# Products of constants in three idle places of TensorE, and the sample scores of the decay attention bound behind the fourth pair's first work

## The chip, the cores and the metric

The program runs on one core of one Trainium2 chip. Its engines work side by side, each through a queue of its own in program order: TensorE (PE; its weight loads are listed as PEld), VectorE (DVE), ScalarE (ACT), GpSimd (POOL), and SyncE (SP), which here only issues DMA transfers. The metric is the device time of one execution in microseconds (us), the median over runs. The profile also gives TensorE's granted clock, as a share of full speed: it is seen at two levels, 1.0 (2.4 GHz) and 0.5 (1.2 GHz).

## The reference

One encoder layer in fp32 for two requests that share weights: a prompt of 1024 tokens, and a sample of 64 tokens that comes with caches (256 past tokens of attention, 256 memory tokens, recurrent states). Model width is 1024. Cut to its frame:

```python
x = layer_norm(x)
proj = x @ w_in                                   # three mixers read the same projection
mixed = concat(gla(...), s5(...), fox(...)) @ w_mix_out
x = layer_norm(alpha * x + mixed)
x = layer_norm(alpha * x + mem_attend(x, mem_k, mem_v, w_q, w_o))
x = layer_norm(alpha * x + conv_ffn(x, w_up, conv_w, conv_b, w_down))
```

and the mixer that matters here, the decay attention (8 heads of 64):

```python
s = einsum('bqhd,bkhd->bhqk', q, k) * 64 ** -0.5
s = s + F[q] - F[k]                               # F: cumulative log-forget values
s = where(k_pos <= q_pos, s, -inf)
out = einsum('bhqk,bkhd->bqhd', softmax(s), v)
```

The sample's 64 queries attend to 256 cached keys and their own 64. All the prompt's and sample's outputs, new keys, values and states are returned.

## The kernel before

**Precision and stages.** fp32 products are made from rounded parts: `mm3` (L198) issues three products hi x hi, hi x lo, lo x hi. A weight tile is loaded raw by SP (L117), rounded by ACT (L118, `_hi`), and the remainder is taken by DVE or POOL (L119, `_lo`). In order of time the stages are: input and memory projections, GLA and S5 (to about 415 us), decay attention (415 to 570), mixing projection with its norm (560 to 680), memory attention (690 to 912), its output projection, the up-projection (to about 1440), and the down-projection.

**Decay attention.** The prompt's eight heads go as four pairs, p = 0 to 3 (z is the head in the pair), each in eight query tiles i of 128. A tile has scores `fx_s` (L983, L984, with the diagonal mask added as a product of `maskb` by `identb`, a bf16 identity, L986), a DVE reduction that adds the decay and finds the extreme value (L989), ACT's exponential (L991), transposes `fx_t` (L998), their copies `fx_pt` (L1000, L1002), products with V `fx_po` (L1007), and an ACT copy to `mixT` (L1009). V of a pair is loaded by L965. After a pair's tiles, `fx_rl` (L1015) spreads the reciprocal row sums and L1017 multiplies `mixT` by them.

**Sample scores.** `fox_sample` is a generator: the code calls it once at p = 2 for its loads (`FsD` and `qk` through SP, L912 and L915) and for the addition of a mask to the decay values (L917, DVE), and then at p = 3, tiles 0, 2, 4 and 6, once for each pair of sample heads: `fs_s` (12 products on L925 to L927), reduction L929, exponential L931, scaling L932 and L933, transposes `fs_t` (L936), `fs_o` (L942), copy to `mixT` (L944).

**Mixing projection.** `residual` adds `mixT` times `w_mix_out` to x, in two stages of 512 inputs. A stage has four weight tiles, u = 0 to 3; a token tile takes 24 products `ps_o`, six for each u. Its input x is loaded into `Xa` and `Xb` (L1078) over the storage that the decay attention used. `bo` holds the rounded parts of `mixT` (L1041, L1042); after stage 0 DVE adds the sums to x (L1057), after stage 1 a norm follows, which squares on ACT (L139) over the tile of sums, and transposes x into features (`ps_tr`, L189).

**Memory attention.** `mem_sample(h)` runs one head of the sample: `ms_s` (L1139), softmax (L1098 to L1102), transposes `ms_t` (L1144), `ms_o` (L1150).

**Order and banks.** The instructions' order on every engine is made by a scheduler that simulates the program; `tc.issue_after` binds an instruction behind another without a wait. TensorE's sums live in eight banks: tag D (two buffers of two banks: `fx_s`, `ps_o`), tag T (two of one: `fx_t`, `m_s`), and tags E and F, one bank each, given in turn by

```python
def pse(name="pse", tag=None):
    turn[0] ^= 1
    return psum.tile([128, 512], F32, tag=tag or "EF"[turn[0]], name=name)
```

unless the caller names one (`fs_*` always E; `fx_po` and `fx_rl` always F).

## Time and profile before

| what | value |
|---|---|
| median of 3 runs | 1747.13 us (1738.27 to 1749.47) |
| the profiled execution | 1746.15 us, span 1744.4 us |
| mean granted TensorE clock | 0.979 |
| busy share of the span | PE 95%, DVE 61%, ACT 40%, POOL 40% |
| PE, products | 10856 |
| chain of waits that ended last | PE 44%, DVE 8%, issue 4%, POOL, ACT and DMA 2% each |

The busy share is an average over stages. A row of a timeline gives the start, the duration, the engine, the line and operation, and in brackets how long the engine had been idle before it and what ended that. "x4" groups four instructions in a row; products of one group overlap, so the spacing from start to start is what one costs. The chain of waits follows the end of the program backwards and gives each step's engine.

### The profile page before, as it was taken

The page shows a single profiled execution, that of the slowest core. Times are in us where ns is not written, and L with a number is a line of the kernel's source. Part 1 is how long each engine was busy: PE and PEld are TensorE (multiplying, and loading weights), DVE is VectorE, ACT ScalarE, POOL GpSimd, SP SyncE. Part 2 cuts the span into 40 slices and gives each one's busy share as a digit, 9 for nine tenths or more (in the row PEclk, how much of TensorE's full clock was granted, in tenths as well). Part 3 has the DMA queues.
Part 4 walks back from the last instruction along what each step waited for, and adds up shares of the span by engine and source line. Part 5 has one row for each costly group of instructions (what it writes and reads, how often), then busy time and mean ns, then how long its engine had stood idle before and what let it go on. Part 6 is the DMA issues. An engine that isn't in the chain of part 4 may idle for free.

```text
span 1744.4 us, 27851 instructions
## 1 busy us (share of the span) xinstructions
PE 1651.9 (95%) x10856; PEld 1451.6 (83%) x10856; DVE 1057.6 (61%) x1806; ACT 695.3 (40%) x1280; POOL 698.9 (40%) x748
## 2 busy tenths in 40 slices
PE   7799998998999999999989899999999998999997
PEld 5699986777777878998778799999999997767775
DVE  8754522674556236124445999778888876775547
ACT  6412224423555135225336654444444446121111
POOL 4454833020010267113223375545455547653323
PEclk9799999999999999999999899999999999999999
DMA  9640233438941311122112122222222226531112
GB/s 329 253 77 27 78 104 110 160 96 225 262 118 47 131 48 37 39 63 69 37 49 78 71 64 90 80 81 80 75 75 81 75 94 256 188 106 37 48 53 99
DMA packets 95753, 178.29 MB, mean 102 GB/s; under 512 B 26206, under 2 KB 48574, under 8 KB 95494
## 3 DMA queue, kind: packets, MB, share of 16 engines
q1 hardware_dynamic: 67910, 142.82, 26.9%
q10 hardware_dynamic: 27712, 33.70, 5.4%
q8 instruction: 85, 1.39, 0.3%
q14 instruction: 46, 0.38, 0.1%
HBM read 129.56 MB, written 46.34 MB: 101 GB/s over the span
## 4 chain that ended last, share of the span: by engine, by line
PE 44%; DVE 8%; issue 4%; POOL 2%; ACT 2%; DMA 2%; POOLq 0%; SPq 0%; DVEq 0%; ACTq 0%
PE u_a L1414 7%; PE ps_d L198 7%; PE u_d L1414 6%; PE u_c L1414 6%; PE ps_a L216 6%; PE ps_o L198 5%; PE u_b L1414 3%; PE m_o L198 1%; POOL wd_lo L119 1%; PE m_s L198 1%; DVE Yb L1580 1%; DVE y L1487 1%; DVE Ya L1580 1%; DMA hraw<-hD 1%; DMA kv_p<-out_mem_v_p 1%
## 5 line engine op out<-in xcount | busy, mean ns | idle before, releaser
L198 PE MATMUL ps_d<-wd_hi,hb 128*128 128x512 f32 x704 | 225.1, 396 | 11.3 <-DVE Ya L1580 3.5
L198 PEld LDWEIGHTS ps_d<-wd_hi,hb 128*128 128x128 f32 x704 | 132.1, 188 | 47.9 <-DVE Yb L1580 3.9
L1414 PE MATMUL u_a<-x2A,wu_wlo 128*128 128x288 f32 (+1 forms) x1032 | 138.6, 290 | 2.7 <-DVE x2A L1225 2.0
L198 PE MATMUL ps_d<-wd_lo,hb 128*128 128x512 f32 x352 | 139.0, 395 | 1.3 <-POOL wd_lo L119 1.3
L1414 PEld LDWEIGHTS u_a<-x2A,wu_wlo 128*128 128x128 f32 x1032 | 133.4, 192 | 3.3 <-DVE x2A L1225 2.4
L198 PE MATMUL ps_o<-wo_hi,bo 128*128 128x512 f32 x384 | 126.5, 403 | 3.0 <-ACT ps_o L139 2.7
L1360 POOL TENSOR_TENSOR wu_wlo<-wu_raw,wu_wlo 128x512 fp32r<-128x512 f32 x63 | 97.2, 1546 | 79.9 <-ACT wu_wlo L1359 79.9
L1487 DVE SCALAR_TENSOR_TENSOR y<-x2B,ffp,y 128x1024 f32<-128x1024 f32 x88 | 125.9, 1431 | 1.1 <-ACT y L1485 1.1
L1517 POOL TENSOR_TENSOR hb<-hraw,hb 128x1024 fp32r<-128x1024 f32 (+1 forms) x40 | 64.9, 1640 | 84.6 <-ACT hb L1516 84.6
L1360 POOL TENSOR_TENSOR wu_whi<-wu_whi 128x512 fp32r<-128x512 f32 x44 | 70.5, 1602 | 60.8 <-ACT wu_whi L1359 60.1
L198 PE MATMUL ps_b<-wb_hi,x0h 128*128 128x512 f32 (+2 forms) x256 | 89.5, 350 | 1.0 <-ACT fv_st L264 1.0
L1359 ACT ACTIVATE wu_wlo<-wu_raw 128x512 fp32r<-128x512 f32 x86 | 54.1, 631 | 90.7 <-DVE wu_raw L1356 39.3
L198 PEld LDWEIGHTS ps_o<-wo_hi,bo 128*128 128x128 f32 x384 | 72.7, 191 | 20.0 <-ACT ps_o L139 3.1
L198 PE MATMUL ps_b<-wb_lo,x0h 128*128 128x512 f32 (+2 forms) x256 | 88.4, 346 | 0.4 <-POOL wb_lo L119 0.4
L198 PE MATMUL ps_b<-wb_hi,x0l 128*128 128x512 f32 (+2 forms) x256 | 88.6, 346 | 0.0
L1580 DVE TENSOR_TENSOR Ya<-Ya,ps_d 128x1024 f32<-128x1024 f32 (+1 forms) x50 | 60.9, 1218 | 44.6 <-PE ps_d L198 39.1
L1042 POOL TENSOR_TENSOR bo<-mixT,bo 128x512 fp32r<-128x512 f32 (+1 forms) x18 | 22.7, 1273 | 151.6 <-ACT bo L1041 151.6
L119 POOL TENSOR_TENSOR wo_lo<-wo_raw,wo_hi 128x1024 fp32r<-128x1024 f32 x14 | 33.2, 2383 | 118.5 <-ACT fx_pt L1000 45.6
L198 PEld LDWEIGHTS ps_d<-wd_lo,hb 128*128 128x128 f32 x352 | 66.1, 188 | 16.9 <-POOL wd_lo L119 2.2
L119 POOL TENSOR_TENSOR wa_lo<-wa_raw,wa_hi 128x1024 fp32r<-128x1024 f32 x16 | 39.2, 2454 | 101.0 <-ACT wa_hi L118 67.8
L198 PE MATMUL ps_o<-wo_lo,bo 128*128 128x512 f32 x192 | 77.1, 402 | 1.1 <-POOL wo_lo L119 1.1
L1516 ACT ACTIVATE hb<-hraw 128x1024 fp32r<-128x1024 f32 (+1 forms) x40 | 25.3, 653 | 128.5 <-PE ps_d L198 116.2
(560 smaller groups left out, 4473.6 us busy)
## 6 DMA issues: line engine op xcount, KB each, us to landing
wu_raw<-in_w_up SPq DMA_DIRECT2D x88, 256.0 KB, 2.8
hD<-y ACTq DMA_DIRECT2D x22, 512.0 KB, 2.6
wd_raw<-in_w_dn SPq DMA_DIRECT2D x22, 512.0 KB, 3.5
hraw<-hD SPq DMA_DIRECT2D x20, 544.0 KB, 4.7
fx<-qk SPq DMA_DIRECT2D x28, 256.0 KB, 8.8
fxk<-qk SPq DMA_DIRECT2D x20, 256.0 KB, 4.8
wa_raw<-in_w_a SPq DMA_DIRECT2D x8, 512.0 KB, 3.7
stage<-in_w_mv SPq DMA_DIRECT2D x8, 512.0 KB, 8.4
```

The costliest lines, as they stand in the source:

```text
L119: (eng or G).tensor_tensor(out=lo[:, :n], in0=raw[:, :n], in1=hi[:, :n].bitcast(F32), op=SUB)
L198: PE.matmul(out, lhsT=lhs[i], rhs=rhs[j], start=start and n == 0, stop=stop and n == 2)
L216: PE.matmul(ps[:, c, 0:272], lhsT=w[i][:, k, :], rhs=xs[j][:, k, t0:t0 + 272], start=k == 0 and n == 0, stop=k == KD - 1 and n == 2)
L1042: G.tensor_tensor(out=sl, in0=part, in1=sh.bitcast(F32), op=SUB)
L1359: S.activation(out=WU[n][0], in_=RAW[n], func=AF.Copy)
L1360: (eng or G).tensor_tensor(out=WU[n][1], in0=RAW[n], in1=WU[n][0].bitcast(F32), op=SUB)
L1414: PE.matmul(ps, lhsT=w[i][:, k, :], rhs=x[j][:, k, c], start=start and k == 0 and q == 0, stop=k == 3 and q == 2, skip_group_check=True)
L1487: V.scalar_tensor_tensor(out=out, in0=u[:, c + j:c + j + n], scalar=cw[j][:, m:m + 1], in1=out, op0=MUL, op1=ADD)
L1516: S.activation(out=t[:, hi:hi + n], in_=r, func=AF.Copy)
L1517: G.tensor_tensor(out=t[:, lo:lo + n], in0=r, in1=t[:, hi:hi + n].bitcast(F32), op=SUB)
L1580: V.tensor_tensor(out=x, in0=x, in1=p, op=ADD)
```

## The change

A helper `fill` issues n products of `identb` by itself (128 weights, 384 columns, bf16) into a bank, without a reader. It is used in three places: 14 into the unused columns of the first `fx_po` bank, bound behind the last scores of the first pair's tile 3; 12 into a new `pse` tile named `fill`, between token tiles 1 and 2 of stage 1 of the mixing projection; 14 into the unused columns of `ms_t` of the last sample head. In `fox_sample` the mask's addition is bound behind the reduction of the fourth pair's tile 0, the first `fs_s` product of each head behind the `fx_po` of that tile, and the generator is advanced in tiles 1, 3, 5 and 7 of the fourth pair instead of 0, 2, 4 and 6. Since `fill` takes a turn of `pse`, later users of E and F swap banks.

Lines move: L917 becomes L929, L925 L937, L942 L954, L983 L995, L989 L1001, L1007 L1024, L1015 L1032, L1017 L1034, L1078 L1097, L198 L208, L189 L199, L117 L127; the fills are L92.

```diff
--- before.py
+++ after.py
...
@@ -78,10 +78,20 @@
         return psum.tile([128, 512], F32, tag="T", name=name, bufs=2)
 
     turn = [0]
+    pins = {}
 
     def pse(name="pse", tag=None):
         turn[0] ^= 1
         return psum.tile([128, 512], F32, tag=tag or "EF"[turn[0]], name=name)
+
+    def fill(out, n, behind=None):
+
+        c = out.shape[1] // 128
+        with tc.issue_after(behind.ins) if behind else nullcontext():
+            for _ in range(n):
+                ins = PE.matmul(out.rearrange("p (a c) -> p a c", a=c), lhsT=identb, rhs=bc(identb, 1, c), start=True, stop=True,
+                                skip_group_check=True)
+                pins.setdefault("fill", ins)
 
     def slot(shape, dtype, name):
         return mem.tile(shape, dtype, tag="sp", name=name, bufs=4)
@@ -195,7 +205,7 @@
 
     def mm3(out, lhs, rhs, start, stop):
         for n, (i, j) in enumerate(PASSES):
-            PE.matmul(out, lhsT=lhs[i], rhs=rhs[j], start=start and n == 0, stop=stop and n == 2)
+            pins["o"] = PE.matmul(out, lhsT=lhs[i], rhs=rhs[j], start=start and n == 0, stop=stop and n == 2)
 
     def mm2(out, stack, w, start, stop):
 
@@ -914,15 +924,17 @@
             for j, src in enumerate((qk[z], qk[2], qk[3])):
                 SY.dma_start(out=q3[j][64 * z:64 * z + 64], in_=src.rearrange("(h d) t -> d h t", d=64)[:, :, TP:T])
             V.memset(PS[z][:, 320:384], 0.0)
-        V.tensor_tensor(out=SF[:, :, 256:320], in0=SF[:, :, 256:320], in1=bc(smask, 1, 4), op=ADD)
         yield
+        with tc.issue_after(pins["mn", 3, 0].ins):
+            V.tensor_tensor(out=SF[:, :, 256:320], in0=SF[:, :, 256:320], in1=bc(smask, 1, 4), op=ADD)
         for p in range(4):
             P, PT = PS[p % 2], PTS[p % 2]
             s = pse("fs_s", "E")
             for z in range(2):
                 h = 2 * p + z
                 o = s[64 * z:64 * z + 64]
-                PE.matmul(o[:, 0:256], lhsT=q3[0][:, h, :], rhs=KC[:, h, :], start=True, stop=True)
+                with tc.issue_after(pins["po", 3, 0].ins):
+                    PE.matmul(o[:, 0:256], lhsT=q3[0][:, h, :], rhs=KC[:, h, :], start=True, stop=True)
                 PE.matmul(o[:, 256:320], lhsT=q3[0][:, h, :], rhs=q3[1][:, h, :], start=True, stop=False)
                 PE.matmul(o[:, 256:320], lhsT=q3[0][:, h, :], rhs=q3[2][:, h, :], start=False, stop=True)
             mn, l = small([128, 1], "fx_mn", bufs=4), small([128, 1], "fs_l", bufs=2)
@@ -967,7 +979,7 @@
         for i in range(8):
             if p == 2 and i < 4:
                 SY.dma_start(out=mixT[:, i, :], in_=mixD[128 * i:128 * i + 128, :])
-            if p == 3 and i % 2 == 0:
+            if p == 3 and i % 2 == 1:
                 next(fs, None)
             n = 128 * (i + 1)
             npc = 1 if n <= 512 else 2
@@ -981,12 +993,12 @@
                     ks = slice(w * c, w * c + w)
                     diag = c == npc - 1
                     PE.matmul(s[:, c, 0:w], lhsT=QS[z][:, qs], rhs=KH[z][:, ks], start=True, stop=False)
-                    PE.matmul(s[:, c, 0:w], lhsT=QS[z][:, qs], rhs=KL[z][:, ks], start=False, stop=not diag)
+                    pins["s"] = PE.matmul(s[:, c, 0:w], lhsT=QS[z][:, qs], rhs=KL[z][:, ks], start=False, stop=not diag)
                     if diag:
                         PE.matmul(s[:, c, w - 128:w], lhsT=identb, rhs=maskb, start=False, stop=True)
                 mn = small([128, 1], "fx_mn", bufs=4)
                 v = P[:, 0:n].rearrange("p (c k) -> p c k", c=npc)
-                V.tensor_tensor_reduce(out=v, in0=s[:, 0:npc, 0:w], in1=fb[:, z, 0:n].rearrange("p (c k) -> p c k", c=npc),
+                pins["mn", p, i] = V.tensor_tensor_reduce(out=v, in0=s[:, 0:npc, 0:w], in1=fb[:, z, 0:n].rearrange("p (c k) -> p c k", c=npc),
                                        scale=1.0, scalar=3.0e38, op0=ADD, op1=MIN, accum_out=mn)
                 S.activation(out=P[:, 0:n], in_=P[:, 0:n], func=AF.Exp, bias=mn, scale=-1.0,
                              accum_out=l[:, 2 * i + z:2 * i + z + 1])
@@ -1002,10 +1014,15 @@
                         V.tensor_copy(out=pt[:, k0:k0 + nk, :], in_=ps[:, 0:nk, :])
                 pts.append(pt)
             o = pse("fx_po", "F")
+            if p == 0 and i == 0:
+                fill(o[:, 128:512], 14)
+            if p == 0 and i == 3:
+                tc.add_manual_dep(pins["fill"].ins, pins["s"].ins.name, mybir.DependencyInfo(
+                    mybir.DependencyClass.NoSync, mybir.DependencyReason.DATA), reason="order")
             for k in range(i + 1):
                 for z in range(2):
-                    PE.matmul(o[64 * z:64 * z + 64, 0:128], lhsT=Vp[:, k, 64 * z:64 * z + 64],
-                              rhs=pts[z][:, k, :], start=k == 0, stop=k == i)
+                    pins["po", p, i] = PE.matmul(o[64 * z:64 * z + 64, 0:128], lhsT=Vp[:, k, 64 * z:64 * z + 64],
+                                                 rhs=pts[z][:, k, :], start=k == 0, stop=k == i)
             S.activation(out=mixT[:, 4 + p, qs], in_=o[:, 0:128], func=AF.Copy)
         V.reciprocal(out=l, in_=l)
         V.tensor_copy(out=le, in_=bc(l, 2, 64))
@@ -1041,6 +1058,8 @@
                     S.activation(out=sh, in_=part, func=AF.Copy)
                     G.tensor_tensor(out=sl, in0=part, in1=sh.bitcast(F32), op=SUB)
                     ops.append((i, m, psd("ps_o"), sh, sl, st))
+                if norm and not tail and stage == 1 and grp[0] == 2:
+                    fill(pse("fill")[:, 0:384], 12, pins["o"])
                 for u in range(4):
                     w = [x.rearrange("p (c n) -> p c n", c=2) for x in us[u]]
                     for i, m, ps, sh, sl, st in ops:
@@ -1136,10 +1155,13 @@
         kvs = caches[h]
         s = pse("ms_s")
         for d in range(2):
-            PE.matmul(s[0:64, 0:256], lhsT=qf[:, 2 * h + d, TP:T], rhs=kvs[:, 0, d, :], start=d == 0, stop=d == 1)
+            ms = PE.matmul(s[0:64, 0:256], lhsT=qf[:, 2 * h + d, TP:T], rhs=kvs[:, 0, d, :], start=d == 0, stop=d == 1)
         P = prob()
         softmax(s[0:64, 0:256].rearrange("p (i c) -> p i c", i=1), P[0:64, 0:1], 64, 1)
-        pt = pse("ms_t").rearrange("p (m c) -> p m c", m=4)
+        pt = pse("ms_t")
+        if h == 3:
+            fill(pt[:, 128:512], 14, ms)
+        pt = pt.rearrange("p (m c) -> p m c", m=4)
         for mt in range(2):
             PE.transpose(pt[:, mt, 0:64], P[0:64, 0, 128 * mt:128 * mt + 128], ident[0:64, 0:64])
         pts = mem.tile([128, 2, 64], F32, tag="misc", name="ms_pt")
```

DVE's queue at the end of the second pair before, where `fxs` and `fxt` are the storage of the sample's scores and the ISA rows are the reductions with their read-out:

```order
L989 ISA fx_3877,fx_mn<-fx_s,fx_3877 128x896
L989 ISA fx_mn 128x1
L917 TENSOR_TENSOR fxt<-fxt,fxs 128x4x64
L989 ISA fx_3877,fx_mn<-fx_s,fx_3877 128x1024
L989 ISA fx_mn 128x1
L1002 COPY fx_pt<-fx_t 128x512
```

and after the change, DVE's queue where the fourth pair begins:

```order
L1027 RECIPROCAL fx_l<-fx_l 128x16
L1028 COPY fxt<-fx_l 128x1024
L1001 ISA fx_3877,fx_mn<-fx_s,fx_3877 128x128
L1001 ISA fx_mn 128x1
L929 TENSOR_TENSOR fxt<-fxt,fxs 128x4x64
L1014 COPY fx_pt<-fx_t 128x512
L1014 COPY fx_pt<-fx_t 128x384
L1014 COPY fx_pt<-fx_t 128x512 x2
L1014 COPY fx_pt<-fx_t 128x128
L1034 TENSOR_TENSOR mixT<-mixT,fx_rl 128x512 x2
L941 ISA fxs,fx_mn<-fs_s,fxt 128x320
```

The addition has moved from between the second pair's reductions to behind the fourth pair's first ones, and the first sample group's reduction (L941) now stands ahead of those of the fourth pair's tile 1.

TensorE's queue around the last `fs_o`, with the tail of the fourth pair, before:

```order
L998 MATMUL fx_t<-ident,fx_3877 128x128 x4
L942 MATMUL fs_o<-fxt,fxs 64x64 x6
L1007 MATMUL fx_po<-fx_pt,fx_3877 64x128 x3
L998 MATMUL fx_t<-ident,fx_3877 128x128 x3
L198 MATMUL ps_o<-wo_hi,bo 128x512
L998 MATMUL fx_t<-ident,fx_3877 128x128 x4
L1007 MATMUL fx_po<-fx_pt,fx_3877 64x128
L998 MATMUL fx_t<-ident,fx_3877 128x128 x3
```

and after:

```order
L948 MATMUL fs_t<-ident,fxs 128x128 x3
L1010 MATMUL fx_t<-ident,fx_3877 128x128 x4
L1024 MATMUL fx_po<-fx_pt,fx_3877 64x128
L1010 MATMUL fx_t<-ident,fx_3877 128x128 x4
L954 MATMUL fs_o<-fxt,fxs 64x64 x6
L1024 MATMUL fx_po<-fx_pt,fx_3877 64x128 x15
L208 MATMUL ps_o<-wo_lo,bo 128x512
L208 MATMUL ps_o<-wo_hi,bo 128x512 x2
```

The last `fs_o` has moved from 13 rows ahead of the pair's last `fx_po` to directly in front of it. SP's queue has its loads of `Xa`, which wait for that `fs_o`, ahead of the weights `wo_raw` in both versions.

TensorE's queue in stage 1 of the mixing projection after the change, where the new fills stand (the pair of rows L92 comes twelve times):

```order
L208 MATMUL ps_o<-wo_hi,bo 128x512 x2
L208 MATMUL ps_o<-wo_lo,bo 128x512
L208 MATMUL ps_o<-wo_hi,bo 128x512
L92 LDWEIGHTS identb
L92 MATMUL fill<-identb 128x384
...
L208 MATMUL ps_o<-wo_hi,bo 128x512
L208 MATMUL ps_o<-wo_lo,bo 128x512
L208 MATMUL ps_o<-wo_hi,bo 128x512 x2
```

In the code the fills come between token tiles 1 and 2; in the queue 135 of the stage's `ps_o` products stand ahead of them, and transposes of the first two normalised tiles too. The other two groups of fills stand in the queue where the code puts them: behind the scores of tile 3 (ahead of its last mask product), and directly behind the last `ms_s`, ahead of `ms_t`.

## Rows read from the trace of the kernel before

**Rows 1.** Table of stretches: us, busy PE, PEld, DVE, ACT, POOL, PEclk, DMA share, GB/s.

```profile
423.90:430.70 6.80, 5.22 (x28) 4.36 (x28) 1.81 (x4) 2.39 (x6) 0.00 (x0) 0.51 1.04 257
481.90:488.70 6.80, 6.26 (x35) 4.65 (x35) 3.34 (x7) 2.48 (x4) 0.00 (x0) 0.50 1.05 229
638.90:642.90 4.00, 4.00 (x12) 3.12 (x11) 2.64 (x2) 2.46 (x2) 2.50 (x4) 0.58 0.02 4
657.50:662.50 5.00, 5.00 (x25) 4.12 (x23) 3.15 (x6) 4.39 (x6) 2.67 (x7) 1.00 0.00 0
908.30:915.10 6.80, 5.48 (x18) 4.36 (x19) 2.32 (x6) 2.44 (x7) 1.96 (x2) 0.51 0.23 77
1456.00:1462.00 6.00, 4.17 (x20) 3.17 (x19) 5.56 (x7) 3.98 (x5) 0.98 (x2) 1.00 1.00 393
```

**Rows 2.** Timeline of TensorE (start, us, engine, line, idle before), start of the decay attention.

```profile
421.28 0.23 PE L986 MATMUL fx_s<-maskb,identb 128*128 128x128 bf16 x1
...
425.48 0.70 PE L1007 MATMUL fx_po<-fx_pt,fx 128*64 128x128 f32 x4 [3.96 <-DMA fx<-out_fox_v_p]
```

**Rows 3.** Timeline of TensorE, score products 384 wide.

```profile
431.53 0.34 PE L984 MATMUL fx_s<-fxk 128*128 128x384 f32 x1
...
431.71 0.33 PE L983 MATMUL fx_s<-fxk 128*128 128x384 f32 x1
```

**Rows 4.** Timeline of all engines, from the second pair to the third.

```profile
476.72 0.23 PE L986 MATMUL fx_s<-maskb,identb 128*128 128x128 bf16 x1
...
481.50 0.43 DVE L917 TENSOR_TENSOR fxt<-fxt,fxs 128x256 f32<-128x256 f32 x1 [7.29 <-DMA fxt<-FsD]
...
482.44 1.09 PE L925 MATMUL fs_s<-fxs,fxt 128*64 128x256 f32 x2 [5.05 <-issue]
...
490.55 0.36 PE L983 MATMUL fx_s<-fxk 128*128 128x256 f32 x1
```

**Rows 5.** Timeline of TensorE, from the first pair to the second.

```profile
442.87 0.23 PE L986 MATMUL fx_s<-maskb,identb 128*128 128x128 bf16 x1
...
447.24 0.36 PE L983 MATMUL fx_s<-fx 128*128 128x256 f32 x1
```

**Rows 6.** Timeline of TensorE, one group of sample scores.

```profile
553.14 0.59 PE L925 MATMUL fs_s<-fxs,fxt 128*64 128x256 f32 x2
...
554.24 0.22 PE L927 MATMUL fs_s<-fxt 128*64 128x64 f32 x1
...
559.49 0.50 PE L936 MATMUL fs_t<-ident,fxs 128*128 128x128 f32 x3
```

**Rows 7.** Timeline of all engines, end of the fourth pair and start of the projection.

```profile
562.74 2.24 SPq L1078 DMA_DIRECT2D Xa<-hd  x5
...
569.46 1.96 PE L1007 MATMUL fx_po<-fx_pt,fx 128*64 128x128 f32 x30
...
569.90 6.18 SPq L117 DMA_DIRECT2D wo_raw<-in_w_mix  x3
...
573.41 1.06 ACT L118 ACTIVATE wo_hi<-wo_raw 128x1024 fp32r<-128x1024 f32 x1 [1.67 <-DMA wo_raw<-in_w_mix]
...
574.24 1.05 PE L1015 MATMUL fx_rl<-ident,fxt 128*128 128x128 f32 x8
...
574.50 1.22 DVE L119 TENSOR_TENSOR wo_lo<-wo_raw,wo_hi 128x1024 fp32r<-128x1024 f32 x1 [4.24 <-ACT wo_hi L118]
```

**Rows 8.** Tile Xa, its loads.

```profile
DMA to landing us min/median/max: 4.2/6.1/6.9
```

**Rows 9.** Timeline of TensorE, second stage of the projection.

```profile
637.55 0.50 PE L198 MATMUL ps_o<-wo_hi,bo 128*128 128x512 f32 x1 [2.66 <-ACT ps_o L139]
```

**Rows 10.** Timeline of TensorE, the last sample head of the memory attention.

```profile
907.92 0.31 PE L1144 MATMUL ms_t<-ident,m_p 64*128 64x64 f32 x2 [3.18 <-DVE m_l L1101]
...
908.83 1.97 PE L1150 MATMUL ms_o<-ms_pt,m_cr 128*128 128x64 f32 x8 [0.60 <-DVE ms_pt L1146]
...
912.44 0.80 PE L204 MATMUL ps_o<-wo_hi,bo 128*128 128x512 f32 x1 [0.78 <-POOL bo L1042]
```

More of the change, by code (lines that the diff above doesn't have):

```diff
@@ L1 @@
 import math
-from contextlib import ExitStack
+from contextlib import ExitStack, nullcontext
 import concourse.bass as bass
```

## The prediction

> **What bounds the kernel now.** TensorE was busy for 95% of the span, so I looked for the places where it stands still or runs at the lower of its two clock levels. I read the table of stretches first, because it puts busy time and granted clock side by side; the timeline of TensorE around each low stretch next, for the idle gap ahead of it and what ended that gap; then the queues that the change touches. The table [rows 1] is to be read by its PEclk column. Four stretches stand at 0.50 to 0.58, which is 1.2 of 2.4 GHz, while TensorE is busy for nearly all the time after its gap: 423.9 to 430.7, 481.9 to 488.7, 638.9 to 642.9 and 908.3 to 915.1. Each follows a gap of more than 2.5 us. The stretch from 1456 us has 1.83 us without a product and stays at 1.00. So in this trace a long gap costs twice: the gap itself, and the products after it at half speed. The fills (products of the constant identb) attack the second cost, the tie of the sample scores attacks a gap. I cost the places as A (start of the decay attention), D (sample scores), B (second stage of the mixing projection), C (last memory sample head).
>
> **A, start of the decay attention.** The last scores of the first four tiles end with the mask at 421.28; the first fx_po starts at 425.48, after 3.96 us for the load of V [rows 2]. Fourteen fills go between. No product of this shape with bf16 operands is in the trace; the nearest are the 128x384 score products, 0.175 us apart start to start [rows 3], so I take 14 x 0.175 = 2.45 us. That leaves 4.2 - 2.45 = 1.75 us idle, near the 1.83 us that cost no clock [rows 1]. The fills delay one mask product, whose reduce nobody waits for before V lands; V's landing hides that, and it would cost 2.45 us if V came at 421. Gain if the clock holds: half of the 5.22 us of busy time in the low stretch [rows 1], 2.6 us. If it does not hold: 0. I take 2.6.
>
> The rows show idle time ahead of each drop, but not whether products whose result nobody reads count. The Trainium skill (TensorE: Matmul & The Clock Gate, Part 1) says that throttled is the default state and that TensorE's activity releases it, which makes no distinction by what is computed. By that rule A and C give their whole sum; without it they give nothing, which is the first rival. No run here shows it yet.
>
> **D, the sample scores.** Before, DVE's addition L917 stands in DVE's queue ahead of the reduces of the second pair's last tile. It waits 7.29 us for the load of FsD, until 481.50; TensorE then waits behind it, 5.05 us, and its fs_s products start at 482.44 at half clock [rows 4]. From the mask of the second pair's last scores to the first 256-wide score of the third pair takes 490.55 - 476.72 = 13.83 us [rows 4]. The same boundary between the first and second pair takes 447.24 - 442.87 = 4.37 us [rows 5]; that between third and fourth also 4.37. Bound behind the fourth pair, both the addition and the products leave this place: 9.46 us off the path. The third pair's own loads do not end any wait there before, and that is all the trace says of what comes next.
>
> What comes back: (1) The first group of 12 fs_s products has to run elsewhere, at full clock 1.1 us (553.14 to 554.24) [rows 6]. (2) In the fourth pair the sample group now starts a tile later and its reduce stands ahead of the reduces of tile 1; the PE order has little between them. No row shows this; bounds 0 and 4 us (another boundary like [rows 5]); I take 1.5, since most of a group still lies among other products. (3) The last fs_o moves to the very end of the attention, and this is where I expect the largest loss. SP's loads of Xa wait for the last fs_o: it was issued at 562.74, and behind it on the same queue the first load of mixing weights (wo_raw, for the third quarter u2 of stage 0) at 569.90 [rows 7]. In the new order only 15 fx_po follow the last fs_o. Those took from 569.46 to 571.4 [rows 7], so on the old clock Xa is issued at 569.5; its five issues take 2.24 us, and wo_raw goes at 571.7 with 2.5 MB in front of it. The last Xa issue is at about 571.3, Xa's slowest landing took 6.9 us [rows 8], so Xa is in at 578.2; with about 1.1 us for its own 0.5 MB (an estimate from the 2.5 MB of Xa in some 7 us) the weights land at 579.3, against 573.4 before. ACT's rounding takes 1.06 us and DVE's remainder 1.22 us behind it [rows 7]: 580.4 and 581.6. TensorE reaches u2 after 22 more products (512 wide: 0.175 x 512 / 384 = 0.23 us each by [rows 3]) and two groups of fx_rl, which took 1.05 us at 574.24 [rows 7], some 0.8 of it ahead of the next product: 578.1. It gets one product in after the rounded weights and then waits for the remainder: a loss of about 3.0 us (581.6 less 578.1 less two products). The bounds are 0 (if Xa's transfers leave room) and 5 (if the wait also drops the clock, as the 2.66 us of [rows 9] did). D in sum: -9.46 + 1.1 + 1.5 + 3.0 = -3.9 us, with ends at -8.4 and +0.6.
>
> **B, mixing projection.** The gap to fill is at 634.89 to 637.55, 2.66 us, ended by ACT's squares releasing a score bank [rows 9]; the low stretch behind it holds 4.0 us of products, of which half, up to 2.0 us, could be won [rows 1]. But the fills write a tile of their own, which takes the E bank that the transposes of the first two normalised tiles use, and in the new order they stand behind these: after 135 products of stage 1, more than five tiles in. On the old clock that is the stretch around 660 us, where TensorE is busy for 5.00 of 5.00 us at full clock [rows 1]. There 12 x 0.175 = 2.1 us are simply added, and the gap at 635 stays. I take +2.1; the ends are +2.1 and -2.0 (as intended).
>
> **C, last memory sample head.** TensorE waits 3.18 us for the softmax before ms_t at 907.92; ms_o then takes 1.97 us and the products from 912.44 on run at half speed until 915.1 [rows 10]. The fills stand in the gap in the new order: 2.45 of 3.18 us, starting when the bank of ms_t has been copied out, so at most some 0.3 us late. The gain if the clock holds: half of 1.97 + 2.66 = 2.3 us, less 0.3: -2.0. The ends are +0.3 (clock falls all the same) and -2.7 (half of all 5.48 us busy [rows 1]).
>
> **Sum.** -2.6 - 3.9 + 2.1 - 2.0 = -6.4 us against the profiled execution's 1746.15 us: 1739.7, rounded to 1740. That execution is 1 us below the median of the runs, 1747.13, and the runs themselves spread over 11 us, so less than 1% (17.5 us) is about what a measurement here cannot tell from no change.
>
> **Rivals.**
> 1. The fills do not hold the clock. For: each leaves some idle time beside it, up to 1.75 us. Against: 1.83 us passed at 1.00. Only D and B remain, C's delay added: 1746.15 - 3.9 + 2.1 + 0.3 = 1744.7.
> 2. No stall at the mixing weights. Xa and the weights share their engines better than I think. For: wo_raw alone landed in 3.5 us (569.90 to 573.41 [rows 7]). Against: one queue, with Xa ahead. Without the 3.0: 1736.7.
> 3. The gap of D only changes its owner. The third pair's start meets the loads for the fourth pair and the sample, at a DMA share of 1.05 [rows 1]; if the boundary takes 9 instead of 4.37 us, D gives +0.8: 1744.4.
> 4. Slower: a sample group's chain lies bare where the new order puts it. From a group's last fs_s (554.24) to its transposes (559.49) takes 5.25 us [rows 6], through DVE and ACT; in the old run the scores and transposes of other tiles filled that. Now the first group stands in tile 1, which has few products of its own, and the last in tile 7, with none behind. If both lie bare, the price is 2 x 5.25 = 10.5 us where the forecast has 1.5. It decides from 7.9 us on, the forecast's 6.4 us of gain and its 1.5. Then 1746.15 - 6.4 - 1.5 + 10.5 = 1748.8. For: DVE's reduce of the first group stands ahead of those of tile 1. Against: in the new order some 30 products stand between the last group's scores and its transposes, and tile 2's scores behind the first group.
> 5. B stands where it was meant to, and everything else as in the forecast: 1739.7 - 4.1 = 1735.6. Against: the order of instructions.
>
> **How the numbers follow.** Forecast 0.45, rival 1 0.15, rival 2 0.18, rival 3 0.12, rival 4 0.07, rival 5 0.03. The range goes from 1731 (rivals 2 and 5 together, 1736.7 - 4.1 = 1732.6, and C's far end) to 1748 (rivals 1 and 3 together reach 1744.7 + 4.6 = 1749; rival 4 lies just outside). Faster by over 1% means below 1729.7, which not even all good ends together reach but for the spread of runs: 0.07. Slower by over 1% means above 1764.6, which no case reaches: 0.03. Within 1%: 0.90.
>
> **What the new profile would show.** A: PEclk 1.00 from 425 to 431, and the same gap shorter by the fills. D: no wait of DVE for FsD at the end of the second pair, fx_s of the third pair's second tile some 9 us earlier against its mask; a wait of TensorE for wo_lo or wo_hi at u2 near 570. B: L92 rows amid dense ps_o products, and a low stretch after the 2.7 us gap as before. C: ms_o near 1.0 us. I am wrong if the clock falls behind A or C, if u2 finds its weights ready, or if the fourth pair's tiles 0 to 2 show waits of more than 4 us in sum.

## The result and the profile after

The changed kernel takes 1758.05 us (median of 7 runs, 1756.36 to 1765.58) against 1746.64 us of the kernel before (7 runs beside them): ratio 1.008, 95% interval 1.006 to 1.0101. It is 0.8% slower; 0.4% faster was forecast (1740 us), and the time lies above the stated range (1731 to 1748 us). The profiled execution after took 1756.36 us, 10.2 us more than the one before.

Its page, the span and TensorE's busy time:

```profile
span 1754.6 us, 27929 instructions
...
PE 1657.9 (94%) x10896; PEld 1452.5 (83%) x10896; DVE 1055.3 (60%) x1806; ACT 696.1 (40%) x1280; POOL 698.9 (40%) x748
```

TensorE is busy for 6.0 us longer than before (1651.9), and the other 4.2 us of the longer span are idle time. The way to find where is to follow the same instructions in both timelines of TensorE. The last column is what each stretch added:

| instruction | before, us | after, us | after less before | added here |
|---|---|---|---|---|
| first mask of the decay attention | 415.94 | 413.33 | -2.61 | -2.6 |
| first pair's last mask | 442.87 | 438.51 | -4.36 | -1.8 |
| second pair's last mask | 476.72 | 480.52 | +3.80 | +8.2 |
| third pair's first 256-wide score | 490.55 | 484.89 | -5.66 | -9.5 |
| fourth pair's last mask | 559.42 | 557.97 | -1.45 | +4.2 |
| first dense `ps_o` behind the pair | 571.35 | 574.57 | +3.22 | +4.7 |
| first addition to `Xa` (DVE) | 582.96 | 592.74 | +9.78 | +6.6 |
| last row of `ms_s` | 903.67 | 916.03 | +12.36 | +2.6 |
| eighth `ps_o` behind the last `ms_o` | 915.47 | 925.62 | +10.15 | -2.2 |

The first row lies ahead of every edit. There the stretch from 356 to 362 us stood at 0.50 in the execution before and at 1.00 in the one after, with the same work: such differences come and go between executions. Over the fifteen profiles of this document (before, after and thirteen experiments) the first mask stands anywhere from 410.80 to 419.46 us. Two executions are therefore compared from the first mask on, and from there the change lost 12.8 us.

Five stretches of the profile after, with the columns of [rows 1]:

```profile
423.00:430.00 7.00, 7.00 (x63) 5.72 (x61) 3.86 (x9) 4.24 (x11) 0.00 (x0) 1.00 1.04 245
455.00:461.00 6.00, 6.00 (x32) 4.15 (x34) 1.81 (x4) 1.65 (x6) 0.00 (x0) 0.50 1.03 262
585.00:591.00 6.00, 5.72 (x13) 4.06 (x14) 2.45 (x2) 1.25 (x2) 0.00 (x0) 0.51 1.00 391
648.00:654.00 6.00, 6.00 (x20) 4.71 (x20) 3.81 (x2) 3.04 (x4) 4.12 (x6) 0.72 0.00 0
917.60:924.00 6.40, 4.36 (x29) 2.88 (x29) 4.21 (x11) 3.99 (x14) 2.83 (x3) 1.00 0.52 164
```

The first row answers to the stretch at 423.9 of [rows 1]: with the fills in front, 7.00 us of work at 1.00 instead of 0.51. The last answers to the one at 908.3: 1.00 instead of 0.51. The row at 648 answers to 638.9 and is no better for its fills (0.72 over 6 us). The two rows between are new: half clock at 455 and at 585, in places where the kernel before ran at full clock.

The two places that gained, A (the fills at the start of the decay attention) first (timeline of TensorE):

```profile
418.69 2.45 PE L92 MATMUL fx_po<-identb 128*128 128x384 bf16 x14
...
422.84 0.44 PE L1024 MATMUL fx_po<-fx_pt,fx 128*64 128x128 f32 x4 [1.65 <-DMA fx<-out_fox_v_p]
```

The row of the fourteen fills lasts 2.45 us. From start to start they are 0.163 us apart, and the mask product behind them starts 2.28 us after the first. The idle time left is 1.65 us instead of 3.96 [rows 2]. C, the fills of the last memory sample head:

```profile
917.65 2.44 PE L92 MATMUL ms_t<-identb 128*128 128x384 bf16 x14 [0.55 <-ACT qf L1202]
...
920.88 1.10 PE L1172 MATMUL ms_o<-ms_pt,m_cr 128*128 128x64 f32 x8 [0.52 <-DVE ms_pt L1168]
```

`ms_o` takes 1.10 us instead of 1.97 [rows 10]. The boundary from the second to the third pair, which answers to [rows 4]:

```profile
480.52 0.23 PE L998 MATMUL fx_s<-maskb,identb 128*128 128x128 bf16 x1
...
484.89 0.36 PE L995 MATMUL fx_s<-fxk 128*128 128x256 f32 x1
```

From the second pair's last mask to the third pair's first 256-wide score it takes 4.37 us, exactly the other boundary's time [rows 5]; the wait for FsD is gone.

B, the fills of the mixing projection, with the gap that they were for:

```profile
647.48 0.50 PE L208 MATMUL ps_o<-wo_hi,bo 128*128 128x512 f32 x1 [2.66 <-ACT ps_o L149]
...
671.12 2.13 PE L92 MATMUL fill<-identb 128*128 128x384 bf16 x12
```

The gap of 2.66 us stands as in [rows 9], and the twelve fills follow 24 us later, amid dense products, for 2.13 us.

**The first new loss** is in the second pair, a stretch that no edit names (timeline of all engines):

```profile
438.76 3.56 SPq L127 DMA_DIRECT2D wo_raw<-in_w_mix  x2
...
450.89 1.06 ACT L128 ACTIVATE wo_hi<-wo_raw 128x1024 fp32r<-128x1024 f32 x1 [6.25 <-DMA wo_raw<-in_w_mix]
...
453.36 1.06 ACT L128 ACTIVATE wo_hi<-wo_raw 128x1024 fp32r<-128x1024 f32 x1 [1.42 <-DMA wo_raw<-in_w_mix]
...
454.33 0.58 ACT L1012 ACTIVATE fx_pt<-fx_t 128x512 f32<-128x512 f32 x1
...
454.96 1.12 PE L1010 MATMUL fx_t<-ident,fx 128*128 128x128 f32 x4 [6.29 <-ACT fx_pt L1012]
```

To be read from the bottom: TensorE stood 6.29 us for ACT's copy of transposes (L1012), and that copy stood in ACT's queue behind the two roundings `wo_hi` of the mixing weights (L128), whose loads SP had issued at 438.76. The order of ACT's queue had changed. Before:

```
L991 ACTIVATE fx_3877,fx_l<-fx_3877,fx_mn 128x256
L118 ACTIVATE wo_hi<-wo_raw 128x1024
L1009 ACTIVATE mixT<-fx_po 128x128
L1000 ACTIVATE fx_pt<-fx_t 128x512
L118 ACTIVATE wo_hi<-wo_raw 128x1024
```

and after:

```
L1003 ACTIVATE fx_3877,fx_l<-fx_3877,fx_mn 128x128
L128 ACTIVATE wo_hi<-wo_raw 128x1024 x2
L1012 ACTIVATE fx_pt<-fx_t 128x512
L1003 ACTIVATE fx_3877,fx_l<-fx_3877,fx_mn 128x256
```

Before, the copy and the 256-wide exponential behind it stood ahead of the first rounding; after, they stand behind both.

**The second new loss** is in the fourth pair. Waits of TensorE in its first three tiles:

```profile
528.92 1.16 PE L1032 MATMUL fx_rl<-ident,fxt 128*128 128x128 f32 x8 [0.78 <-DVE mixT L1034]
...
530.93 0.44 PE L1024 MATMUL fx_po<-fx_pt,fx 128*64 128x128 f32 x4 [0.85 <-DVE mixT L1034]
...
533.45 0.44 PE L995 MATMUL fx_s<-fx 128*128 128x384 f32 x1 [0.94 <-DVE fx_mn L1001]
```

These three are 2.6 us, and no wait in the pair is longer than 0.94 us. Before, the pair had none over 0.15 us; after, such waits are 3.6 us in sum up to its last mask and 1.1 us from there to the first dense `ps_o`. The two rows of the table come to 8.9 us, 8.7 of them behind the third pair's last mask. The 4.0 us that are not waits are busy time at full clock: 1.5 us more in `fs_s`, whose first group stood at the boundary behind the second pair before, and the rest in `fx_t`, `fx_po` and `fx_rl`, which are the same products standing further apart.

**The third** is at the mixing weights (all engines; the first row is the pair's last products with V, which answer to 569.46 in [rows 7]):

```profile
572.73 1.91 PE L1024 MATMUL fx_po<-fx_pt,fx 128*64 128x128 f32 x29
...
572.92 2.25 SPq L1097 DMA_DIRECT2D Xa<-hd  x5
...
575.28 0.85 SPq L127 DMA_DIRECT2D wo_raw<-in_w_mix  x2
...
584.14 1.06 ACT L128 ACTIVATE wo_hi<-wo_raw 128x1024 fp32r<-128x1024 f32 x1 [9.19 <-DMA wo_raw<-in_w_mix]
...
585.23 2.49 DVE L129 TENSOR_TENSOR wo_lo<-wo_raw,wo_hi 128x1024 fp32r<-128x1024 f32 x2 [2.71 <-ACT wo_hi L128]
...
585.25 1.22 PE L208 MATMUL ps_o<-wo_hi,bo 128*128 128x512 f32 x2 [3.52 <-ACT wo_hi L128]
```

SP issues Xa at 572.92, wo_raw behind it at 575.28; the rounding waits 9.19 us for the load, and TensorE 3.52 us for the rounding. The half clock behind it is the row at 585 above.

### The profile page after: what moved, and what is told of

Its sections match the earlier page's. It is cut to its first block, busy times and chain, and to the rows that moved or that the text cites. A ratio compares the mean times of both kernels' runs of the same rounds, so it can differ in the third digit from the quotient of the medians.

```text
span 1754.6 us, 27929 instructions
## 1 busy us (share of the span) xinstructions
PE 1657.9 (94%) x10896; PEld 1452.5 (83%) x10896; DVE 1055.3 (60%) x1806; ACT 696.1 (40%) x1280; POOL 698.9 (40%) x748
## 4 chain that ended last, share of the span: by engine, by line
PE 43%; DVE 7%; issue 3%; POOL 2%; ACT 2%; DMA 2%; POOLq 0%; DVEq 0%; SPq 0%; ACTq 0%
PE u_a L1436 7%; PE ps_d L208 7%; PE u_d L1436 6%; PE u_c L1436 6%; PE ps_o L208 5%; PE ps_a L226 5%; PE u_b L1436 3%; PE m_o L208 1%; PE m_s L208 1%; POOL wd_lo L129 1%; DVE Yb L1602 1%; DVE y L1509 1%; DVE Ya L1602 1%; DMA hraw<-hD 1%; POOL wo_lo L129 0%
## 5 line engine op out<-in xcount | busy, mean ns | idle before, releaser
L208 PE MATMUL ps_d<-wd_hi,hb 128*128 128x512 f32 x704 | 225.1, 396 | 11.1 <-DVE Ya L1602 3.0
L208 PEld LDWEIGHTS ps_d<-wd_hi,hb 128*128 128x128 f32 x704 | 132.1, 188 | 47.7 <-DVE Yb L1602 3.9
L208 PE MATMUL ps_d<-wd_lo,hb 128*128 128x512 f32 x352 | 139.1, 395 | 1.3 <-POOL wd_lo L129 1.3
L208 PE MATMUL ps_o<-wo_hi,bo 128*128 128x512 f32 x384 | 128.9, 408 | 7.6 <-ACT wo_hi L128 3.5
L208 PEld LDWEIGHTS ps_o<-wo_hi,bo 128*128 128x128 f32 x384 | 73.8, 193 | 25.5 <-ACT wo_hi L128 3.7
L208 PE MATMUL ps_b<-wb_hi,x0h 128*128 128x512 f32 (+2 forms) x256 | 89.9, 352 | 1.0 <-ACT fv_st L274 1.0
L208 PE MATMUL ps_b<-wb_lo,x0h 128*128 128x512 f32 (+2 forms) x256 | 89.2, 349 | 0.4 <-POOL wb_lo L129 0.4
L208 PE MATMUL ps_b<-wb_hi,x0l 128*128 128x512 f32 (+2 forms) x256 | 89.2, 349 | 0.0
L208 PEld LDWEIGHTS ps_d<-wd_lo,hb 128*128 128x128 f32 x352 | 66.1, 188 | 17.0 <-POOL wd_lo L129 2.2
L208 PE MATMUL ps_o<-wo_lo,bo 128*128 128x512 f32 x192 | 78.0, 406 | 1.3 <-POOL wo_lo L129 1.3
```

Of the source, the lines that this page charges most:

```text
L208: pins["o"] = PE.matmul(out, lhsT=lhs[i], rhs=rhs[j], start=start and n == 0, stop=stop and n == 2)
```

## The experiments

Every ratio is that to the runs of the kernel before on the same chip. "us" is the ratio applied to its 1746 us. The expectations are stated as times, so the medians stand beside it: that of the run, and that of the kernel before measured with it.

| run | median, us | median before, us | ratio | 95% interval | us against before |
|---|---|---|---|---|---|
| e1_A_alone | 1752.1 | 1745.75 | 1.0012 | 0.9988 to 1.0036 | +2 |
| e2_A_pinned | 1746.9 | 1745.75 | 1.0001 | 0.9978 to 1.0024 | 0 |
| e3_D_alone | 1753.62 | 1745.75 | 1.0035 | 1.0017 to 1.0053 | +6 |
| e4_D_third | 1741.5 | 1745.75 | 0.9977 | 0.9955 to 0.9999 | -4 |
| e5_B_bank_T | 1744.06 | 1745.88 | 0.9988 | 0.9973 to 1.0003 | -2 |
| e6_D_1246 | 1742.62 | 1745.88 | 0.9984 | 0.9964 to 1.0005 | -3 |
| e7_D_swap | 1747.57 | 1745.88 | 1.0008 | 0.9991 to 1.0026 | +1 |
| e8_mended | 1737.42 | 1745.88 | 0.9938 | 0.9922 to 0.9955 | -11 |
| e9_change_mended | 1741.74 | 1746.56 | 0.9971 | 0.9956 to 0.9986 | -5 |
| e10_mended_no_A | 1732.87 | 1746.56 | 0.9912 | 0.9888 to 0.9936 | -15 |
| e11_mended_no_pin | 1744.88 | 1746.56 | 0.9982 | 0.9964 to 1.0000 | -3 |
| e12_mended_again | 1732.0 | 1747.73 | 0.9924 | 0.9899 to 0.9949 | -13 |
| e13_no_A_again | 1734.77 | 1747.73 | 0.9929 | 0.9905 to 0.9953 | -12 |

e1 is the run where the two differ most: its medians are 6.4 us apart, its ratio gives 2, with an interval of 4 us to either side.

My theory after the result: the fills at A move ACT's roundings forward; the late sample groups cost the fourth pair and, through Xa, the mixing weights. The rival put these losses down to the other edit each time. Runs e1 to e4 take the edits apart.

**A alone (e1).** The change without B, C and the bound sample scores:

```diff
-                if norm and not tail and stage == 1 and grp[0] == 2:
-                    fill(pse("fill")[:, 0:384], 12, pins["o"])
...
-        if h == 3:
-            fill(pt[:, 128:512], 14, ms)
```

> Only the fills at the start of the decay attention; nothing else of the change. Theory 1 (the fills change ACT's order: its two roundings of the mixing weights stand earlier, in the second pair, and wait there for their load): a gap of about 6 us on TensorE in the second pair that ends with a copy of transposes on ACT, some 8 us lost there against 2 us gained by the clock at the start; the boundary between second and third pair then hides most of the loss, since TensorE waits there for a load whose time does not depend on it; total 1744 to 1751 us. Theory 2 (the gap in the second pair belongs to the bound sample scores): no gap in the second pair, total about 1745 us, the boundary as before.

TensorE and DVE in the second pair and at its end:

```profile
459.90 1.12 PE L1008 MATMUL fx_t<-ident,fx 128*128 128x128 f32 x4 [6.21 <-ACT fx_pt L1010]
...
486.10 0.43 DVE L927 TENSOR_TENSOR fxt<-fxt,fxs 128x256 f32<-128x256 f32 x1 [5.59 <-DMA fx<-qk]
...
486.78 0.43 PE L1022 MATMUL fx_po<-fx_pt,fx 128*64 128x128 f32 x2 [3.03 <-DVE fx_pt L1012]
```

The gap is there without any bound score (6.21 us). From the first pair's last mask to the last mask but one of the second pair this execution took 7.5 us more than the one before. At the boundary TensorE's wait is 3.03 us where it was 5.05 [rows 4], and of the 8.2 us by which it was late, 2.6 were gone at the third pair. So the new order of ACT comes with A, and in this kernel the wait for the sample's loads hides a part of what it costs. (The row puts the end of DVE's wait to a load of `fx`; the second load of FsD, which the addition reads, landed at 485.66, 0.44 us before it.) The median, 1752.1 us, lies 1 us above the expectation.

**A with ACT's roundings bound (e2).**

```diff
-        S.activation(out=hi[:, :n], in_=raw[:, :n], func=AF.Copy)
+        with tc.issue_after(behind.ins) if behind else nullcontext():
+            S.activation(out=hi[:, :n], in_=raw[:, :n], func=AF.Copy)
```

with `behind` the ACT copy of tile 5 of the second pair.

> The fills at the start of the decay attention, and ACT's roundings of the mixing weights bound behind the copy of tile 5 of the second pair, so that they cannot stand earlier. Theory 1: no gap in the second pair, which starts and ends about 2 to 4 us earlier than before; the boundary to the third pair, where TensorE waits for the load of FsD, takes back most of that; total 1742 to 1747 us. Theory 2: the same as the run with the fills alone.

```profile
477.69 0.43 DVE L928 TENSOR_TENSOR fxt<-fxt,fxs 128x256 f32<-128x256 f32 x1 [12.96 <-DMA fx<-qk]
...
478.37 0.69 PE L1023 MATMUL fx_po<-fx_pt,fx 128*64 128x128 f32 x2 [10.40 <-DVE fx_pt L1013]
```

No gap in the second pair. It came to its last mask but one 7.6 us earlier than in the execution before, and the boundary took it back: DVE waited 12.96 us there, TensorE 10.40, until 478.37 (the second load of FsD landed at 477.24). The third pair began 2.5 us early in an execution that had entered the attention 3.7 us early. So what was gained ahead of the boundary is worth nothing while the sample's loads set it.

**The bound scores alone (e3).** The change without A, B and C.

> Only the bound sample scores, with the generator advanced in tiles 1, 3, 5, 7; no fills. Theory 1: no gap in the second pair; the boundary between second and third pair 9 us shorter; the fourth pair about 8 us longer; TensorE waits about 3.5 us for the mixing weights at u2 and runs some 6 us at half clock behind that; total 1748 to 1754 us. Theory 2: the fourth pair's loss belongs to the fills, total about 1740 us.

Second pair, then the mixing weights:

```profile
457.38 0.43 PE L1019 MATMUL fx_po<-fx_pt,fx 128*64 128x128 f32 x2 [2.73 <-ACT mixT L1021]
```

```profile
575.51 0.85 SPq L127 DMA_DIRECT2D wo_raw<-in_w_mix  x2
...
584.23 1.06 ACT L128 ACTIVATE wo_hi<-wo_raw 128x1024 fp32r<-128x1024 f32 x1 [9.04 <-DMA wo_raw<-in_w_mix]
...
585.34 1.22 PE L208 MATMUL ps_o<-wo_hi,bo 128*128 128x512 f32 x2 [3.38 <-ACT wo_hi L128]
```

Counted here and below to the third pair's last mask, the boundary is 9.3 us shorter; from there the fourth pair is 4.1 us longer up to its last mask and 4.7 us behind that, and the wait at u2 and its clock cost 6.5 us. Total +6 us. The fills have no part in these losses. The wait of 2.73 us in the second pair has ACT's order of before: the load landed 14.1 us after its issue (442.01 to 456.11) instead of 12.4.

**Where the sample groups stand (e4).** Bound behind the third pair instead, and advanced in tiles 0, 2, 4, 6:

```diff
-        with tc.issue_after(pins["mn", 3, 0].ins):
+        with tc.issue_after(pins["mn", 2, 7].ins):
...
-                with tc.issue_after(pins["po", 3, 0].ins):
+                with tc.issue_after(pins["po", 2, 7].ins):
...
-            if p == 3 and i % 2 == 1:
+            if p == 3 and i % 2 == 0:
```

> No fills; the addition of the mask to the sample's decay values bound behind the third pair's last reduction and the first sample products behind the third pair's last products with V, the generator advanced in tiles 0, 2, 4, 6 as before. Theory 1 (what costs is the place of the sample groups in the fourth pair, not their removal from the second): boundary 9 us shorter, 1 us back for the moved group, the last fs_o as far from the end as before, no wait at u2; total 1736 to 1740 us. Rival (the saved wait comes back as another wait at the third pair): within 2 us of before.

The boundary keeps its 9.3 us, the fourth pair still grows by 4.0 us up to its last mask, and behind it takes 12.07 us where it took 11.93 before and 16.6 in the change. No wait at u2. Total -4 us; the median of 1741.5 us lies above the expected 1736 to 1740. Of the 4 us in the fourth pair I had counted only the first group's products, 1.1 us.

**Only the last group early (e6).** `i in (1, 2, 4, 6)` in place of `i % 2 == 1`, scores bound as in the change:

> Only the bound sample scores, but the generator advanced in tiles 1, 2, 4, 6 of the fourth pair: the first group stands as late as in the change, the last as early as before. Theory 1 (the last fs_o, through the loads of Xa ahead of the mixing weights, makes TensorE wait at u2): no wait at u2 and no low clock there, 6 us better than the run with the bound scores alone, so 1745 to 1749 us; the boundary's 9 us stay won, the fourth pair still 6 to 9 us longer. Rival (the wait at u2 has to do with the shifted start of the pair): wait at u2 as in the bound scores alone.

```profile
555.93 2.30 SPq L1090 DMA_DIRECT2D Xa<-hd  x5
...
563.08 6.81 SPq L127 DMA_DIRECT2D wo_raw<-in_w_mix  x3
...
567.22 1.06 ACT L128 ACTIVATE wo_hi<-wo_raw 128x1024 fp32r<-128x1024 f32 x1 [2.29 <-DMA wo_raw<-in_w_mix]
```

Xa goes at 555.93, the weights at 563.08, the rounding waits 2.29 us and TensorE not at all. The fourth pair costs 7.3 us, its tail nothing (11.93 us). Total -3 us, 9 us better than the bound scores alone, and with 1742.6 us better than the expectation. In the two profiles the second pair alone makes 3.4 us of difference (TensorE waited 0.91 us for ACT there against 2.73), so the place of the last group may be worth less than 9.

**The weights ahead of Xa (e7).** The order of tiles 1, 3, 5, 7, with SP's loads exchanged:

```diff
+    wmix = res_weights("w_mix", 0, (G, V))
     for i in range(NT):
-        SY.dma_start(out=X[i], in_=hd[128 * i:128 * i + 128, :])
+        with tc.issue_after(pins["raw"].ins):
+            SY.dma_start(out=X[i], in_=hd[128 * i:128 * i + 128, :])
```

> The bound sample scores as in the change (tiles 1, 3, 5, 7), but the first two late loads of mixing weights on SP ahead of the loads of Xa, which are bound behind them. Theory 1: the weights for u2 are there in time, no wait at u2, 6 us better than the bound scores alone, 1745 to 1749 us; the fourth pair as long as there. Rival (Xa itself is late then): TensorE waits behind the first addition to Xa, about the same total as the bound scores alone.

```profile
571.48 2.53 SPq L1092 DMA_DIRECT2D Xa<-hd  x5
...
572.18 1.06 ACT L128 ACTIVATE wo_hi<-wo_raw 128x1024 fp32r<-128x1024 f32 x1 [0.76 <-DMA wo_raw<-in_w_mix]
```

The roundings are done by 576.1 and TensorE has no wait at u2, while the pair's tail is as long as in the change (16.6 us). With e6 this shows the chain: last fs_o, Xa, mixing weights, u2. In this execution TensorE waited 5.36 us in the second pair for the roundings in ACT's old order, so the total (+1 us) shows less than this place gained.

**B in a free bank (e5).** `pst("fill")`, tag T, in place of `pse("fill")`:

> Only the 12 fills of the mixing projection, written into a bank of tag T, which nobody holds there, instead of a tile of tags E and F; they stand behind the 48 products of the first two token tiles of stage 1. Theory 1 (the fills of the change stood in the wrong place, and in the right place they hold the clock): no stretch at half clock behind the gap of 2.66 us, 1.5 to 2 us gained there, total 1743 to 1745 us against 1745.7. Rival (fills do not hold the clock here): the low stretch stays, no change.

```profile
640.06 2.12 PE L92 MATMUL fill<-identb 128*128 128x384 bf16 x12
...
642.88 0.51 PE L208 MATMUL ps_o<-wo_hi,bo 128*128 128x512 f32 x1 [0.69 <-ACT ps_o L149]
```

The fills start right behind the 48th product and 0.69 us stay idle; the stretch behind runs at full clock. From the last product ahead of the gap to the 21st behind it this execution took 8.74 us, the one before 10.29: 1.6 us won there, and in total -2 us with an interval that still holds no change. But e1, which has no fills here, had the same gap of 2.66 us, kept the full clock behind it and took 8.74 us too. One pair of profiles does not show what fills do; the count over all of them stands below.

**All mended (e8).** A, C, B in tag T, bound roundings, scores as in e4:

> All three groups of fills, those of the mixing projection in a bank of tag T; ACT's roundings of the mixing weights bound behind tile 5 of the second pair; the sample scores bound behind the third pair's end and advanced in tiles 0, 2, 4, 6. Theory 1: the gains add up: 2 at the start of the attention, 5 from the sample scores, 2 at each of the other fills: 11 us, so 1733 to 1737 us against 1745.7. Rival (a saved wait comes back at the next load, as in the run with pinned roundings): 1739 to 1743 us.

Faster by 0.62% (0.45 to 0.78%), and by 0.76% in the repetition below. The median, 1737.4 us, is just above the expected 1733 to 1737. The second pair has no gap, and the boundary takes 4.37 us.

**The change with three losses undone (e9)** (bound roundings, weights ahead of Xa, tag T; tiles 1, 3, 5, 7):

> The whole change with its order of sample groups (tiles 1, 3, 5, 7), and three losses undone: ACT's roundings bound behind tile 5 of the second pair, the mixing weights for u2 and u3 ahead of Xa on SP, the fills of the mixing projection in a bank of tag T. Theory 1: the change's 1758 us less 8 (second pair), 6 (u2) and 4 (fills: 2 that they cost, 2 that they gain): 1739 to 1742 us. Rival (the losses hide each other): above 1746 us.

1741.74 us, inside the expectation: the three together are worth what was expected of them, and a gain over the kernel before is left. The fourth pair's losses stand in this profile as in the change, 4.0 us up to its last mask and 4.7 behind it.

**The mended kernel without A (e10), and without the bound roundings (e11):**

> The mended kernel without the 14 fills at the start of the decay attention. Theory 1: now that no later load takes the gain back, those fills are worth the 2 to 2.5 us that the stretch shows: about 1739.5 us against the mended kernel's 1737.4. Rival (they are worth nothing in the total): 1737 us.

> The mended kernel with ACT's roundings of the mixing weights free again, so that the fills at the start move them forward in ACT's order. Theory 1: a gap of about 6 us on TensorE in the second pair and low clock behind it; the boundary to the third pair has no wait any more that could hide it: 8 us slower than the mended kernel, 1743 to 1747 us. Rival (the binding does nothing): 1737 us.

Without the bound roundings (e11) TensorE waits again:

```profile
453.65 0.91 PE L1010 MATMUL fx_t<-ident,fx 128*128 128x128 f32 x4 [3.62 <-ACT fx_pt L1012]
```

and the total is 8 to 10 us worse than the mended kernel (0.9982 against 0.9938 and 0.9924). The gap is 3.62 us here and was 6.29: it is set by when the load lands. Without A (e10) the kernel came out faster than with it, against the expectation, though the two intervals overlap. The repetition of both on one chip (e12 with the fills, e13 without):

> The mended kernel once more, beside the one without the fills at the start of the decay attention on the same chip. Theory 1 (the 2.3 us that the stretch shows reach the end): 2 to 3 us faster than that one. Rival (they are lost among what varies from run to run, or taken back): no difference beyond the intervals, or slower.

> The mended kernel without the 14 fills at the start of the decay attention, on the same chip as the run with them. Theory 1: 2 to 3 us slower than that one. Rival: the same within the intervals, or faster as the two earlier calls had it (1732.9 against 1737.4 us).

0.9924 with the fills, 0.9929 without: no difference that can be told. From the first mask of the attention to the first pair's last the fills gave 2.6 us in e8 against e10 and 1.2 us in e12 against e13. Whether that arrives in the total stays open; that the kernel is faster without them did not repeat.

**The second pair in all profiles.** From the first pair's last mask to the last mask but one of the second pair, us, by the order of ACT's queue:

| roundings `wo_hi` | profiles | us |
|---|---|---|
| order of before | before, e3, e4, e5, e6, e7 | 30.78, 34.56, 33.66, 34.43, 31.19, 37.30 |
| moved forward (A, not bound) | after, e1, e11 | 38.94, 38.30, 35.04 |
| bound behind tile 5 | e2, e8, e9, e10, e12, e13 | 29.64 to 29.65 |

The execution before is the shortest of six with its order; up to this place e5's kernel is the same, and took 3.7 us more. Against the mean of the six, 33.7 us, the moved order costs 3.8 us and not 8.2, and binding the roundings gains 4.0 us over that mean, with A and without it. No run binds them alone, so this share of the mended kernel's gain is read from the profiles and not measured in a total.

**The clock behind the three gaps in all profiles.** Profiles with the full clock in the first 3 us behind the gap:

| place | fills in the gap | no fills in the gap |
|---|---|---|
| A, first `fx_po` | 6 of 7 (not e11) | 1 of 8 (e7) |
| B, the gap of 2.66 us | 7 of 7 | 2 of 8 (e1, e3) |
| C, `ms_t` | 7 of 7 | 0 of 8 |

At C the clock fell all the same 3 to 5 us behind `ms_t` in three of the seven (e9, e11, e13). The two exceptions at A are e7 without fills and e11 with them. Each is shown by a row of TensorE's timeline and the row of the stretch behind it, with the columns of [rows 1]:

```profile
421.45 0.44 PE L1019 MATMUL fx_po<-fx_pt,fx 128*64 128x128 f32 x4 [3.13 <-DMA fx<-out_fox_v_p]
...
421.50:428.50 7.00, 7.00 (x63) 5.83 (x64) 4.42 (x10) 5.16 (x13) 0.00 (x0) 1.00 1.04 248
```

```profile
422.66 0.44 PE L1024 MATMUL fx_po<-fx_pt,fx 128*64 128x128 f32 x4 [1.76 <-DMA fx<-out_fox_v_p]
...
422.70:429.70 7.00, 7.00 (x51) 5.72 (x52) 2.85 (x6) 4.13 (x11) 0.00 (x0) 0.76 1.04 256
```

So the fills decide the clock in most executions, not in every one.

## Why the prediction was wrong

**A, the step that failed first.** The sentence that the fills "delay one mask product, whose reduce nobody waits for" put their whole cost at that. They also changed the order that the scheduler made for ACT: its two roundings came to stand ahead of a copy that TensorE needs. Every profile with A and free roundings has that order (after, e1, e11), none without A has it; why the scheduler chose it is not shown. The prediction follows the new order on TensorE, DVE and SP and says nothing of ACT's, and no rival has it. In the two profiles it cost 8.2 us; against the mean of six profiles with the old order it is 3.8 us, because the execution from which the prediction read its rows was the luckiest of them in this place.

**A, its gain.** Sized at 2.6 us, half of the busy time in the low stretch. From the first `fx_po` to the first pair's last mask the execution before took 17.40 us and six of the seven with fills 15.65 to 15.67: 1.7 us. From the first mask, where V's landing comes in, the seven with fills took 24.84 us on average and the eight without 26.13. So 1.3 us is what A gives on average, half of the forecast. The price of a fill, 0.175 us, was 0.163; the row's 2.45 us agree with the forecast only because they include the end of the last product.

**D, the gap.** Right: 9.46 us forecast, 9.46 measured, and the boundary takes 4.37 us in every profile with bound scores, so no other wait took the place (rival 3 did not come).

**D, item 2.** The step that put the fourth pair at 1.1 + 1.5 us, with an upper bound of 4 for the second, failed: 4.2 us up to the last mask and 4.7 us behind it, 8.9 us. Rival 4 had the place and with 10.5 us nearly the size, at a chance of 0.07, but not quite the mechanism: no sample group's chain lies bare for its 5.25 us. The waits are 4.7 us in sum, none over 0.94, and 4.0 us are busy time, of which the prediction had counted 1.1 for the first group. The sign that it gave, more than 4 us of waits in tiles 0 to 2, did not come either: they are 2.6. Tile 7 is the dearer place: with the last group in tile 6 (e4, e6) the 4.7 us behind the last mask vanish, while the rest costs 4 us or more wherever the first group was tried (7.3 in e6).

**D, item 3.** The chain was right, and its wait of 3.0 us came as 3.52; it ended with ACT's rounding, and the remainder was in time. The clock, which I kept only in the upper bound of 5, fell behind it: 0.51 over 6 us, and the stretch cost 6.6 us, above that bound. After my own rows, in which 2.66 us of waiting had dropped the clock, it should have stood in the sum.

**B.** Right: the fills stand in dense work (a row of 2.13 us), the gap and its low clock remain; 2.6 us in all against 2.1.

**C.** Right in this profile: 2.2 us against 2.0. Over all profiles the stretch from the last `ms_s` took 9.7 us on average with fills (seven) and 10.9 without (eight), so 1.3 is what C gives on average. No run has C alone.

**The rule of the Trainium skill** (TensorE: Matmul & The Clock Gate, Part 1), that activity releases the throttle, agrees with the table of clocks above: with products that nobody reads in the gap the full clock stood behind it in 20 of 21 cases, without them in 3 of 24. Rival 1 did not come.

**The sum.** -1.8 + 8.2 - 9.5 + 4.2 + 4.7 + 6.6 + 2.6 - 2.2 = +12.8 us from the attention's start, against -6.4 forecast. Missed: 8.2 at ACT, 6.3 in the fourth pair, 3.6 at the weights; the rest is off by about 1. The range was built from bounds on the terms that I had named, so a term that I had not named could not fall inside it. Its upper end of 1748 us also lay below what the prediction itself gave for rivals 1 and 3 together (1749) and for rival 4 (1748.8). And a change of much less than 1% can be told here: the result's interval is 0.2% to either side.

## What to carry to other kernels

When a scheduler writes the order, an edit on one engine is an edit on all of them: compare the order on every engine, and look first at instructions that wait for a transfer and now stand ahead of something that TensorE needs. Work that is moved off a gap needs a place with cover and a look at what its last instruction releases: here a group of small products in the last tile delayed a load, behind which weights were queued. Filling a gap with products of constants keeps the clock in most executions if their bank is free at that moment; no run with fills alone shows a gain in the total (e2, e5). And look at more than one profile of the kernel before: a wait that is small in one execution can be several us in the next, and a forecast from that one execution inherits its luck.

## What the runs showed that was not expected

The landing time of the two mixing weights' loads, with ACT's order unchanged, moved TensorE's wait in the second pair between 0.37 us (before), 0.91 (e6), 1.80 (e4), 2.56 (e5), 2.73 (e3) and 5.36 us (e7); binding the roundings later removed it. And the clock of a stretch that no edit touched, 356 to 362 us, was 0.50 in one execution and 1.00 in another behind the same gap of 1.24 us, so not every drop follows a long gap; and e7's 3.13 us at A and the 2.66 us at B in e1 and e3 had no drop behind them.
